# A SwiGLU layer's first column block by seven products instead of eight, and one token sum split where it is made

## The chip, the cores and the metric

One core of a Trainium2 chip runs the whole program. The metric is the device time of one execution in microseconds (us), as the median of several runs.

The names of the engines in the profile: PE is TensorE (matmuls and transposes), DVE is VectorE, ACT is ScalarE, POOL is GpSimd, SP is SyncE, which here only issues DMA transfers, in the order of its queue. Every engine takes its own instructions strictly in order: one that waits holds up all that stand behind it on that engine.

## The reference, cut to what matters

```python
x = x + _rmsnorm(merged @ W['w_out'], W['norm_mix_post'])
f = _rmsnorm(x, W['norm_ffn_pre'])
f = (jax.nn.silu(f @ W['w_ffn_gate']) * (f @ W['w_ffn_up'])) @ W['w_ffn_down']
```

The layer runs on 1024 prompt tokens and on 64 sample tokens (`DEC`); the model width is 1024, the FFN width (`D_FF`) 2816. Everything is float32.

## The kernel before

**Operands.** TensorE works on fp32r operands. A float32 matrix is therefore kept as two fp32r parts, hi and lo: `split` copies the matrix to hi on ACT and subtracts hi from it on DVE to get lo. A product is then three matmuls per 128 rows of the inner width: hi by hi, hi by lo and lo by hi. `wino_mm` issues one such product over 512 of the 1024 inner rows, 12 matmuls of 128x512.

**The output stage (`mix_out`)** goes over nine token tiles in the order 8, 0, 4, 1, 5, 2, 6, 3, 7 (tile 8 holds the 64 sample tokens). For each it multiplies by `w_out`, normalizes (`post`), adds the residual, normalizes again (`pre`, whose result is the tile `xn`), transposes `xn` by eight TensorE transposes into two PSUM banks, and splits them into `H`, the FFN's activation operand: `H[:, k, i, t]` with k the inner rows in eights, i hi or lo, t the token. `block(r, c)` is one quarter of it: 512 inner rows, 512 tokens. While a tile pair (t, t+4) goes through, the hooks of `token_sums` form four sums of those quarters on DVE and put each to `tk`, a tensor in DRAM.

**The FFN's first stage (`ffn_in`)** goes over eleven pieces of 256 columns of `w_ffn_gate` and `w_ffn_up`. For pieces 1 to 10, each matrix is multiplied by seven products in the manner of Strassen and Winograd: two take parts of the weights as they are (a11 and a12), four take sums of weight quarters (s1 to s4, made on POOL by `wino_weights` and then split), one takes a22. Three of the token operands are sums too: T2, T3, T4, which `wino_tokens` loads from `tk` and splits; a fourth, t1, stands in the place of `block(0, 1)` in `H`. The sample tokens' 64 columns go along as `decode_rows`, 16 small matmuls of 128x256 per matrix, which read `HD`, an ACT copy of the sample part of `H`.

Piece 0 is done by `ffn_first` as the plain eight products of each matrix: first all of those on `H`'s tokens 0 to 511 (four output tiles, 96 matmuls, tags wx for gate and wz for up), then those on tokens 512 to 1023. Between the two halves `wino_tokens` brings T2, T3, T4, and at the end of piece 0 it brings t1 from `tk` over `block(0, 1)`, which is free from then on.

**Order.** The instruction order of each engine is fixed when the program is built, by a scheduler that works from its own estimates; nothing is reordered on the chip. Pools that follow each other share memory, so a tile of a new pool may have to wait for the last reader of an old one. Loads and stores all go through SP's one queue.

Of the kernel before, what the change touches and what calls it, by code (L numbers as in the profile page):

```python
# [8 lines left out]
F32 = mybir.dt.float32  # L9
# [59 lines left out]
class Net:  # L69
# [54 lines left out]
    def split(self, wh, wl, raw):  # L124
        self.nc.scalar.activation(wh, raw, AF.Copy)  # L125
        self.nc.vector.tensor_sub(wl, raw, wh)  # L126

# [881 lines left out]
    def pre(self, P, x, gb, hi, lo, hook=None):  # L1009

        nc = self.nc
        r = x.shape[0]
        ss = P.tile([128, 4], F32, "ss", "ss")[:r]
        xn = P.tile([128, D], F32, "xn", "xn")[:r]
        nc.scalar.activation(xn, x, AF.Square, scale=1 / 32.0, accum_out=ss[:, 0:1])
        rs = self.rstd(P.pool, ss[:, 0:1])
        nc.vector.scalar_tensor_tensor(xn, x, rs, gb[:r], op0=OP.mult, op1=OP.mult)
        for k0 in (0, 4):
            ps = self.ps.tile([128, 512], F32, name="tr", tag="tr")
            for k in range(4):  # L1020
                nc.tensor.transpose(ps[:, k * 128:k * 128 + r], xn[:, (k0 + k) * 128:(k0 + k + 1) * 128], self.ident[:r, :r])
            self.split(hi[:, k0:k0 + 4], lo[:, k0:k0 + 4], ps.rearrange("p (k t) -> p k t", k=4)[:, :, :r])
            if hook:
                hook(k0 // 4, ps)

    def token_sums(self, P, t):
# [3 lines left out]
        V = nc.vector  # L1030
        x1, y = [None, None], [None]

        def put(n, x):
            nc.sync.dma_start(self.tk[n, :, :, t * 128:(t + 1) * 128], x.rearrange("p (k t) -> p k t", k=4))

# [4 lines left out]
        def second(r, ps):  # L1040
            if not r:
                y[0] = P.tile([128, 512], F32, "t1", "t1")
                V.tensor_sub(y[0], ps, x1[0])
                put(0, y[0])
                return
            t2 = P.tile([128, 512], F32, "t2", "t2")
            V.tensor_sub(t2, ps, y[0])
            put(1, t2)
            V.tensor_sub(x1[0], t2, x1[0])
            put(2, x1[0])  # L1050
            V.tensor_sub(x1[1], x1[1], t2)
            put(3, x1[1])
        return first, second

# [11 lines left out]
    def mix_out(self, P, U):  # L1066
        nc = self.nc
        self.x2 = self.dram.tile([TOK, D], F32, name="x2")
        self.tk = self.dram.tile([4, 128, 4, 512], F32, name="tk")
        gb, gp = self.bcast(P, "norm_mix_post"), self.bcast(P, "norm_ffn_pre")  # L1070
# [24 lines left out]

    def wino_tokens(self, PT, P, first):

        if first:
            T = [self.H[:, 0:4, :, 512:SEQ]]
        else:  # L1100
            T = [PT.tile([128, 4, 2, 512], F32R, name=f"T{n}") for n in (2, 3, 4)]
            two = lambda t: (t[:, :, 0], t[:, :, 1])
            self.B = dict(b11=self.block(0, 0), b21=self.block(1, 0), b22=self.block(1, 1), t1=self.block(0, 1),
                          t2=two(T[0]), t3=two(T[1]), t4=two(T[2]))
        for i in (0,) if first else (1, 0, 2):
            for k in (0, 2):
                t = T[i][:, k:k + 2, 1].bitcast(F32)
                self.nc.sync.dma_start(t, self.tk[i + (not first), :, k:k + 2])
                for j in range(2):
# [4 lines left out]

    def wino_weights(self, P, w, p, i, sums=True):

# [3 lines left out]
        for r in range(2):  # L1120
            x = W.tile([128, 4, 256], F32, name="raw", tag="wraw", bufs=2) if i % 2 == 0 or not sums else P.tile([128, 4, 256], F32, "raw", "raw")
            nc.sync.dma_start(x, w[:, 4 * r:4 * r + 4, p * 256:(p + 1) * 256])
            if not sums and i == r == 1:
                h, l = (P.tile([128, 4, 256], F32R, n, "s") for n in ("wh", "wl"))
            elif (2 * i + r) % 3 < 2:
# [4 lines left out]
            self.split(h, l, x)  # L1130
            raw.append(x)
            D.append((h, l))
        if not sums:
            return D
        a11, a21 = (raw[0][:, :, s:s + 128] for s in (0, 128))
# [13 lines left out]
        return D, dict(a11=h(D[0], 0), a12=h(D[1], 0), a22=h(D[1], 1), s1=s1, s2=s2, s3=s3, s4=s4)  # L1149

    def ffn_first(self, P, w, HD, PT):

        nc = self.nc
        D = [self.wino_weights(P, w[up], 0, up, sums=False) for up in range(2)]
        g = {}
        for c in range(2):
            for up in range(2):
                for n in range(2):
                    ps = self.ps.tile([128, 512], F32, name="w", tag=("wx", "wz")[up])
                    for r in range(2):  # L1160
                        self.wino_mm(ps, tuple(x[:, :, n * 128:(n + 1) * 128] for x in D[up][r]), self.block(r, c), start=r == 0, stop=r == 1, whole=True)
                    if not up:
                        x = g[f"{n + 1}{c + 1}"] = P.tile([128, 512], F32, "c", f"g{n + 1}{c + 1}")
                        nc.scalar.activation(x, ps, AF.Silu)
                    else:
                        x = g[f"{n + 1}{c + 1}"]
                        nc.vector.tensor_mul(x, x, ps)
                if c:
                    Q = self.ps.tile([128, 512], F32, name="wd", tag="wd")[:, :256]
                    self.decode_rows(Q, self.decode_pairs(HD, D[up]), 0, 16)  # L1170
                    self.decode_gate(P, Q, up, 0)
            if not c:
                self.wino_tokens(PT, P, False)
        self.wino_tokens(PT, P, True)
        self.act_sums(0, g, {x: P.tile([128, 512], F32, "c", "u" + x) for x in ("11", "22", "21")})

# [24 lines left out]

    def wino_mm(self, out, a, b, start=False, stop=True, whole=False):

        for k in range(4):
            for i, j in ((0, 0), (0, 1), (1, 0)):
                self.nc.tensor.matmul(out, a[i][:, k], b[j][:, k], start=start and k == i == j == 0,  # L1206
                                      stop=stop and k == 3 and i == 1, skip_group_check=not start and not whole)

    def ffn_in(self, PT, P):
# [9 lines left out]

        self.ffn_first(P, w, HD, PT)  # L1220
        B = self.B
        for p in range(1, 11):
            for up in range(2):
                D, a = self.wino_weights(P, w[up], p, 2 * p + up)
                X, Y, Z = (self.ps.tile([128, 512], F32, name=t, tag=t) for t in ("wx", "wy", "wz"))
                Q = self.ps.tile([128, 512], F32, name="wd", tag="wd")[:, :256]
                dec = self.decode_pairs(HD, D)
                self.wino_mm(X, a["a11"], B["b11"], start=True)
                self.wino_mm(Y, a["a12"], B["b21"], start=True)
                c = {x: P.tile([128, 512], F32, "c", ("u" if up else "g") + x) for x in ("11", "12", "21", "22") if not (up and x == "12")}  # L1230
                A.activation(c["11"], Y, AF.Copy)
                V.tensor_add(c["11"], c["11"], X)
                self.wino_mm(Z, a["s3"], B["t3"], start=True)
                self.wino_mm(X, a["s2"], B["t2"])
                A.activation(c["21"], X, AF.Copy)
                self.decode_rows(Q, dec, 0, 8)
                self.wino_mm(X, a["s1"], B["t1"])
                A.activation(c["22"], Z, AF.Copy)
                V.tensor_add(c["22"], c["22"], X)  # L1239
                self.decode_rows(Q, dec, 8, 16)  # L1240
                self.wino_mm(X, a["s4"], B["b22"])
                self.wino_mm(Z, a["a22"], B["t4"])
                V.tensor_add(c["21"], c["21"], Z)
                self.decode_gate(P, Q, up, p)
                if not up:
                    g = c
                    A.activation(g["12"], X, AF.Silu)
                    for x in ("11", "22", "21"):
                        A.activation(g[x], g[x], AF.Silu)
                    continue  # L1250
                for x in ("11", "22", "12", "21"):
                    V.tensor_mul(g[x], g[x], X if x == "12" else c[x])
                self.act_sums(p, g, c)
            self.down_sums(P, p)
            if p == 5:
# [356 lines left out]
```

## Time and profile before

| | us |
|---|---|
| median of 3 runs | 1753.33 (1753.03 to 1759.03) |
| the profiled execution's own time | 1759.74 |
| its span, first to last instruction | 1758.0 |
| PE busy in the span | 1693.2 (96%) |
| DVE, ACT, POOL busy | 1036.4, 729.7, 520.9 |

PE is busy nearly all the time, so what counts is how much PE has to do and where it stands still. The places of this case lie between 926 us (the last product of the output stage) and 980 us (the first product of piece 1). Start times are in us from the start of the span.

### The profile page before, as it was taken

The page shows a single profiled execution, that of the slowest core. Times are in us where ns is not written, and L with a number is a line of the kernel's source. Part 1 is how long each engine was busy: PE and PEld are TensorE (multiplying, and loading weights), DVE is VectorE, ACT ScalarE, POOL GpSimd, SP SyncE. Part 2 cuts the span into 40 slices and gives each one's busy share as a digit, 9 for nine tenths or more (in the row PEclk, how much of TensorE's full clock was granted, in tenths as well). Part 3 has the DMA queues.
Part 4 walks back from the last instruction along what each step waited for, and adds up shares of the span by engine and source line. Part 5 has one row for each costly group of instructions (what it writes and reads, how often), then busy time and mean ns, then how long its engine had stood idle before and what let it go on. Part 6 is the DMA issues. An engine that isn't in the chain of part 4 may idle for free.

```text
span 1758.0 us, 24713 instructions
## 1 busy us (share of the span) xinstructions
PE 1693.2 (96%) x9092; PEld 1479.8 (84%) x9092; DVE 1036.4 (59%) x1579; ACT 729.7 (42%) x1355; POOL 520.9 (30%) x450
## 2 busy tenths in 40 slices
PE   8999999999999898899999999999999999999998
PEld 6999998988898877798787888888888877888886
DVE  7437916337777767767464655555555456445674
ACT  6431135125555555633344433333333344444542
POOL 2026200012323223224231544445444212001453
PEclk9999999999999989999999999999999999999999
DMA  8362563884444343147445544446444386655332
GB/s 286 92 153 64 126 137 110 249 213 102 105 102 107 70 109 89 56 151 236 144 157 184 164 140 139 146 133 199 140 140 148 109 302 206 205 189 169 106 110 89
DMA packets 220713, 258.23 MB, mean 147 GB/s; under 512 B 26144, under 2 KB 168592, under 8 KB 220576
## 3 DMA queue, kind: packets, MB, share of 16 engines
q1 hardware_dynamic: 219936, 255.20, 48.0%
q0 software_dynamic: 656, 1.44, 0.6%
q8 instruction: 72, 1.18, 0.3%
q14 instruction: 49, 0.40, 0.1%
HBM read 165.32 MB, written 76.51 MB: 138 GB/s over the span
## 4 chain that ended last, share of the span: by engine, by line
PE 75%; DVE 12%; DMA 5%; ACT 3%; issue 3%; POOL 1%; SPq 1%; DVEq 0%; POOLq 0%; ACTq 0%
PE pj L1206 14%; PE tr L1206 8%; PE pj L137 6%; PE pj L139 6%; PE pj L138 6%; PE z L1372 3%; PE z L1206 3%; DVE p L735 3%; PE pj L1372 3%; PE tr L1372 2%; PE av L811 2%; PE z L138 2%; PE z L139 2%; PE z L137 2%; PE tr L781 1%
## 5 line engine op out<-in xcount | busy, mean ns | idle before, releaser
L137 PE MATMUL pj<-H,wh 128*128 128x362 f32 (+3 forms) x648 | 218.4, 337 | 5.9 <-DVE ql L634 3.6
L139 PE MATMUL pj<-H,wl 128*128 128x362 f32 (+3 forms) x648 | 215.8, 334 | 0.6 <-DVE wl L115 0.6
L138 PE MATMUL pj<-H,wh 128*128 128x362 f32 (+3 forms) x648 | 215.4, 333 | 0.0
L126 DVE TENSOR_TENSOR wl<-raw,wh 128x1024 fp32r<-128x1024 f32 x96 | 136.2, 1422 | 113.0 <-ACT wh L125 109.8
L737 POOL TENSOR_TENSOR w<-w,p 128x383 f32<-128x383 f32 (+4 forms) x68 | 92.7, 1373 | 315.2 <-DVE w L739 187.6
L125 ACT ACTIVATE wh<-raw 128x1024 fp32r<-128x1024 f32 x96 | 101.1, 1058 | 112.7 <-PE z L1372 44.4
L137 PEld LDWEIGHTS pj<-H,wh 128*128 128x128 f32 x648 | 123.3, 190 | 7.6 <-DVE ql L634 3.9
L139 PEld LDWEIGHTS pj<-H,wl 128*128 128x128 f32 x648 | 123.1, 190 | 1.5 <-DVE wl L115 1.0
L138 PEld LDWEIGHTS pj<-H,wh 128*128 128x128 f32 x648 | 123.3, 190 | 0.9 <-issue 0.4
L1206 PE MATMUL pj<-H,s 128*128 128x512 f32 x480 | 118.2, 395 | 0.0
L148 POOL TENSOR_TENSOR rs<-rs,mhalf 128x1 f32<-128x1 f32 (+1 forms) x54 | 32.6, 606 | 279.2 <-DVE rs L147 279.1
L1206 PEld LDWEIGHTS pj<-H,s 128*128 128x128 f32 x480 | 89.9, 188 | 20.9 <-DVE c L1239 0.3
L125 ACT ACTIVATE s<-st 128x512 fp32r<-128x512 f32 x80 | 50.3, 629 | 127.6 <-PE pj L1206 116.8
L1140 POOL TENSOR_TENSOR st<-raw 128x512 f32<-128x512 f32 x40 | 61.3, 1532 | 126.4 <-issue 52.3
L126 DVE TENSOR_TENSOR s<-st,s 128x512 fp32r<-128x512 f32 x80 | 64.4, 805 | 41.5 <-ACT s L125 40.9
L119 ACT ACTIVATE wh<-raw 128x1024 fp32r<-128x1024 f32 (+1 forms) x52 | 46.6, 898 | 98.9 <-PE av L138 51.4
L115 DVE TENSOR_TENSOR wl<-raw,wh 128x1024 fp32r<-128x1024 f32 (+1 forms) x50 | 51.0, 1021 | 57.9 <-ACT wh L119 57.8
L785 ACT ACTIVATE wth<-tr 128x512 fp32r<-128x512 f32 (+2 forms) x112 | 50.3, 453 | 83.3 <-PE tr L781 42.8
L786 DVE TENSOR_TENSOR wtl<-tr,wth 128x512 fp32r<-128x512 f32 (+2 forms) x112 | 55.2, 496 | 49.4 <-ACT wth L785 48.9
L733 ACT ACTIVATE p<-z 128x512 f32<-128x512 f32 (+4 forms) x116 | 59.0, 509 | 42.6 <-PE z L835 16.7
L735 DVE TENSOR_TENSOR_SCAN p<-p,zero 128x384 f32<-128x384 f32 (+4 forms) x68 | 73.9, 1094 | 0.2
L1206 PE MATMUL pj<-H,wh 128*128 128x512 f32 x224 | 71.1, 394 | 0.6 <-ACT H L125 0.4
(553 smaller groups left out, 4626.8 us busy)
## 6 DMA issues: line engine op xcount, KB each, us to landing
sd<-c SPq DMA_DIRECT2D x77, 256.0 KB, 3.1
raw<-sd SPq DMA_DIRECT2D x77, 256.0 KB, 2.8
raw<-in_w_in_dram SPq DMA_DIRECT2D x32, 512.0 KB, 5.4
raw<-in_w_ffn_gate_dram SPq DMA_DIRECT2D x22, 512.0 KB, 3.7
raw<-in_w_ffn_up_dram SPq DMA_DIRECT2D x22, 512.0 KB, 4.8
wd<-in_w_ffn_down_dram SPq DMA_DIRECT2D x44, 256.0 KB, 3.4
td<-wd SPq DMA_DIRECT2D x22, 512.0 KB, 3.1
raw<-td SPq DMA_DIRECT2D x44, 256.0 KB, 3.0
```

Of the source, the lines that this page charges most:

```text
L125: self.nc.scalar.activation(wh, raw, AF.Copy)
L126: self.nc.vector.tensor_sub(wl, raw, wh)
L137: self.nc.tensor.matmul(out, wh, xh, start=i == 0, stop=False)
L138: self.nc.tensor.matmul(out, wh, xl, start=False, stop=False)
L139: self.nc.tensor.matmul(out, wl, xh, start=False, stop=i == n - 1)
L733: nc.scalar.activation(p, z, AF.Sigmoid, scale=-1.0)
L735: nc.vector.tensor_tensor_scan(p[:, ::-1], p[:, ::-1], self.zero.to_broadcast([128, n]), 1.0 if carry is None else carry, op0=OP.mult, op1 ...
L737: (nc.gpsimd if e == 'g' else nc.vector).tensor_tensor(w[:, :n - 1], w[:, :n - 1], p[:, 1:], op=OP.mult)
L786: nc.vector.tensor_sub(wl[:, a:b], ps[:, a:b], wh[:, a:b])
L1140: op(t, x, y)
L1206: self.nc.tensor.matmul(out, a[i][:, k], b[j][:, k], start=start and k == i == j == 0, stop=stop and k == 3 and i == 1, skip_group_check=n ...
L1372: nc.tensor.matmul(B[b + n], x[:, 0, c], y[:, 1], start=new and p == j == 0, stop=p == 10 and j == 2, skip_group_check=not new)
```

## The change

Piece 0 is done by the seven products as well. `ffn_in` is cut into `begin` (the products a11 and a12, which need no sums, and the first output) and `end` (the five others). For piece 0 it runs `begin` for gate, `begin` for up, with the decode rows between the two products, then `wino_tokens` and both `end`s. The sum t1 goes no more through `tk`: the second transposes' first half is not split into `H` (`block(0, 1)` itself is not used any more), and the hook of the output stage splits the sum `y` there instead. `tk` holds three sums.

```diff
 def pre(...):
-            self.split(hi[:, k0:k0 + 4], lo[:, k0:k0 + 4], ps...)
+            if not hook or (hook[1], k0) != (True, 0):
+                self.split(hi[:, k0:k0 + 4], lo[:, k0:k0 + 4], ps...)
...
 def second(r, ps):
                 V.tensor_sub(y[0], ps, x1[0])
-                put(0, y[0])
+                self.split(*(self.H[:, 0:4, i, 512 + t * 128:640 + t * 128] for i in range(2)), four(y[0]))
                 return
...
 def wino_weights(...):
-            x = W.tile(..., tag="wraw", bufs=2) if i % 2 == 0 or not sums else P.tile([128, 4, 256], F32, "raw", "raw")
+            x = W.tile(..., tag="wraw", bufs=2) if i % 2 == 0 else P.tile([128, 4, 256], F32, "raw", "raw")
...
-    def ffn_first(self, P, w, HD, PT):
...
 def ffn_in(...):
+        def begin(p, up):
+            D, a = self.wino_weights(P, w[up], p, 2 * p + up)
...
+            self.wino_mm(X, a["a11"], B[0], start=True)
+            if not p:
+                self.decode_rows(Q, dec, 0, 16)
+            late = self.wino_mm(Y, a["a12"], B[1], start=True)
...
+        for p in range(11):
+            if p:
+                g = end(p, 0, *begin(p, 0)[0], None)
+                end(p, 1, *begin(p, 1)[0], g)
+                self.down_sums(P, p)
+            else:
+                S0, _ = begin(p, 0)
+                S1, late = begin(p, 1)
+                with after(self.last_w[0].ins), after(self.last_w[1].ins):
+                    self.wino_tokens(PT)
+                with after(late.ins):
+                    g = end(p, 0, *S0, None)
+                    end(p, 1, *S1, g)
```

How it stands in the instruction order, at three places. In the rows, `pj`, `z`, `tr` and `av` are PSUM banks, `wh` and `wl` weights' hi and lo, and numbers behind a name tell tiles of one name apart.

PE before, around the transposes of token tile 7, the last of the output stage: the rows of `pj<-H` ahead of them are the 48 matmuls of gate on tokens 0 to 511.

```order
L1206 MATMUL pj<-H,wl 128x512
L1206 MATMUL pj<-H,wh 128x512 x2
L1206 MATMUL pj<-H,wl 128x512
L1021 MATMUL tr<-ident,xn 128x128 x8
L1182 MATMUL z<-wh,HD 128x256
```

PE of the change, from the transposes of token tile 3 to those of tile 7 and the first row behind them: here the only matmuls between the two are the 12 of gate's a11.

```order
L1020 MATMUL tr<-ident,xn 128x128 x8
L1174 MATMUL pj<-H,wh 128x512 x2
L1174 MATMUL pj<-H,wl 128x512
L1174 MATMUL pj<-H,wh 128x512 x2
L1174 MATMUL pj<-H,wl 128x512
L1174 MATMUL pj<-H,wh 128x512 x2
L1174 MATMUL pj<-H,wl 128x512
L1174 MATMUL pj<-H,wh 128x512 x2
L1174 MATMUL pj<-H,wl 128x512
L1020 MATMUL tr<-ident,xn 128x128 x8
L1150 MATMUL z<-wh,HD 128x256
```

The transposes of tile 7 stand 36 matmuls earlier in PE's order than before.

SP's queue of the change at the end of the output stage; `T_9637`, `T_9638` and `T_9639` are T2, T3 and T4, and the first `raw<-in_w_ffn_up_dram` are up's weights of piece 0. Gate's weights of piece 0 are issued early in both kernels, and before, up's stood right behind them.

```order
L1035 DMA tk<-t_9440 512x1x128
L1035 DMA tk<-x_9343 512x1x128
L1035 DMA tk<-x_9352 512x1x128
L1106 DMA T_9637<-tk 128x2x512 x2
L1106 DMA T_9638<-tk 128x2x512 x2
L1120 DMA raw<-in_w_ffn_up_dram 128x4x256 x2
L1106 DMA T_9639<-tk 128x2x512 x2
L1120 DMA raw<-in_w_ffn_gate_dram 128x4x256 x2
```

Up's weights of piece 0 now stand behind the puts of tile 7 and behind four of the six loads of the token sums.

ACT of the change from `HD` on; `s<-st` are the splits of the weight sums, `wh<-raw` those of up's weights.

```order
L1183 ACTIVATE HD<-H 128x1024
L125 ACTIVATE s<-st 128x512 x3
L977 ACTIVATE q<-z 64x256
L125 ACTIVATE s<-st 128x512
L1159 ACT_TABLE_LOAD
L1159 ACTIVATE y<-y 64x256
L125 ACTIVATE wh<-raw 128x1024
L1201 ACTIVATE c<-z 128x512
L125 ACTIVATE wh<-raw 128x1024
L125 ACTIVATE T_9638<-T_9638 128x512 x4
L125 ACTIVATE T_9637<-T_9637 128x512 x4
```

Before, `wh<-raw` followed `HD` at once; now gate's weight sums stand ahead of it, and all splits of the token sums behind it.

## Rows read from the trace of the kernel before

**Rows 1.** Busy time by stretch: span, PE, PEld, DVE, ACT, POOL, clock, DMA

```profile
940.00:960.00 20.00, 17.97 (x89) 14.71 (x88) 12.53 (x19) 12.94 (x21) 0.00 (x0) 1.00 0.78 246
1200.00:1400.00 200.00, 200.00 (x946) 165.53 (x945) 113.18 (x137) 74.57 (x124) 88.83 (x76) 1.00 0.45 144
```

**Rows 2.** Chain that ended last, in order of time: start, us, what

```profile
956.45 10.89 PE pj L1206 x48
967.34 11.15 PE tr L1206 x48
978.50 1.80 PE av L1182 x15
```

**Rows 3.** Timeline of PE: start, us, line, what, [idle before <-releaser]

```profile
928.17 0.49 PE L1206 MATMUL pj<-H,wh 128*128 128x512 f32 x1 [0.39 <-ACT H L125]
928.89 0.50 PE L1206 MATMUL pj<-H,wh 128*128 128x512 f32 x1 [0.23 <-DVE H L126]
...
939.68 1.03 PE L1021 MATMUL tr<-ident,xn 128*128 128x128 f32 x8
942.40 0.38 PE L1182 MATMUL z<-wh,HD 128*128 128x256 f32 x1 [1.68 <-ACT HD L1214]
...
980.13 0.62 PE L1206 MATMUL pj<-H,wh 128*128 128x512 f32 x2
```

**Rows 4.** Timeline of DVE, the chain of token tile 7

```profile
934.79 1.28 DVE L1017 SCALAR_TENSOR_TENSOR xn<-xo,rs,gb_norm_ffn_pre 128x1024 f32<-128x1024 f32 x1 [0.73 <-POOL rs L148]
...
942.75 0.68 DVE L1047 TENSOR_TENSOR t<-tr,t 128x512 f32<-128x512 f32 x1
...
944.68 2.35 DVE L126 TENSOR_TENSOR wl<-raw,wh 128x1024 fp32r<-128x1024 f32 x2
```

**Rows 5.** Timeline of ACT, from the transposes of tile 7 on

```profile
940.32 1.09 ACT L125 ACTIVATE H<-tr 128x512 fp32r<-128x512 f32 x2 [6.46 <-PE tr L1021]
941.29 1.06 ACT L1214 ACTIVATE HD<-H 128x1024 fp32r<-128x1024 f32 x1
942.24 2.01 ACT L125 ACTIVATE wh<-raw 128x1024 fp32r<-128x1024 f32 x2
...
952.73 1.15 ACT L125 ACTIVATE T<-T 128x512 fp32r<-128x512 f32 x2 [6.09 <-DMA T<-tk]
954.09 1.16 ACT L125 ACTIVATE T<-T 128x512 fp32r<-128x512 f32 x2 [0.20 <-DMA T<-tk]
...
958.25 1.16 ACT L125 ACTIVATE T<-T 128x512 fp32r<-128x512 f32 x2 [0.20 <-DMA T<-tk]
```

**Rows 6.** Timeline of SP's queue: puts of tile 7, loads of the sums, weights

```profile
943.46 0.51 SPq L1034 DMA_DIRECT2D tk<-t  x1
947.26 1.91 SPq L1108 DMA_DIRECT2D T<-tk  x4
951.19 0.47 SPq L1122 DMA_DIRECT2D raw<-in_w_ffn_up_dram  x1
```

**Rows 7.** Line 1122, weight loads between 860 and 975 us: from issue to landing

```profile
DMA to landing us min/median/max: 3.5/9.9/11.3
```

**Rows 8.** Busy time by stretch, around two idle times of PE (columns as rows 1)

```profile
372.40:375.80 3.40, 0.01 (x1) 0.01 (x1) 0.60 (x2) 1.68 (x6) 0.00 (x0) 0.87 0.92 191
375.80:382.60 6.80, 6.80 (x27) 6.51 (x28) 3.10 (x6) 0.05 (x1) 3.48 (x7) 0.56 0.74 233
...
589.20:592.00 2.80, 0.10 (x2) 0.07 (x2) 2.79 (x6) 1.97 (x5) 1.15 (x2) 1.00 0.89 205
592.00:596.80 4.80, 4.80 (x23) 4.80 (x24) 3.56 (x7) 1.00 (x3) 0.27 (x1) 0.64 0.01 2
```

**Rows 9.** The page's group of POOL's weight sums: count, busy us, mean ns

```profile
L1140 POOL TENSOR_TENSOR st<-raw 128x512 f32<-128x512 f32 x40 | 61.3, 1532 | 126.4 <-issue 52.3
```

More of the change, by code (lines that the diff above doesn't have):

```diff
@@ L1047, in second @@
             V.tensor_sub(t2, ps, y[0])
-            put(1, t2)
+            put(0, t2)
             V.tensor_sub(x1[0], t2, x1[0])
-            put(2, x1[0])
+            put(1, x1[0])
             V.tensor_sub(x1[1], x1[1], t2)
-            put(3, x1[1])
-        return first, second
+            put(2, x1[1])
+        return (first, False), (second, True)
     def rows(self, dst, prompt, sample, t):
@@ L1093, in mix_out, with wino_tokens @@
             self.pre(P, x, gp, *(self.H[:, :, i, c0:c0 + r] for i in range(2)), hook=hooks.get(t))
[L1096 to L1105, printed above, removed]
+    def wino_tokens(self, PT):
+        T = [PT.tile([128, 4, 2, 512], F32R, name=f"T{n}") for n in (2, 3, 4)]
+        two = lambda t: (t[:, :, 0], t[:, :, 1])
+        self.B = dict(b11=self.block(0, 0), b21=self.block(1, 0), b22=self.block(1, 1), t1=self.block(0, 1),
+                      t2=two(T[0]), t3=two(T[1]), t4=two(T[2]))
+        for i in (1, 0, 2):
             for k in (0, 2):
                 t = T[i][:, k:k + 2, 1].bitcast(F32)
-                self.nc.sync.dma_start(t, self.tk[i + (not first), :, k:k + 2])
+                self.nc.sync.dma_start(t, self.tk[i, :, k:k + 2])
                 for j in range(2):
@@ L1120, in wino_weights @@
         for r in range(2):
-            x = W.tile([128, 4, 256], F32, name="raw", tag="wraw", bufs=2) if i % 2 == 0 or not sums else P.tile([128, 4, 256], F32, "raw", "raw")
+            x = W.tile([128, 4, 256], F32, name="raw", tag="wraw", bufs=2) if i % 2 == 0 else P.tile([128, 4, 256], F32, "raw", "raw")
             nc.sync.dma_start(x, w[:, 4 * r:4 * r + 4, p * 256:(p + 1) * 256])
-            if not sums and i == r == 1:
-                h, l = (P.tile([128, 4, 256], F32R, n, "s") for n in ("wh", "wl"))
-            elif (2 * i + r) % 3 < 2:
+            if (2 * i + r) % 3 < 2:
                 h = W.tile([128, 4, 256], F32R, name="wh", tag="whi", bufs=2)
@@ L1129, in wino_weights @@
                 h, l = P.tile([128, 4, 256], F32R, "wh", "dh"), P.tile([128, 4, 256], F32R, "wl", "dl")
-            self.split(h, l, x)
+            self.last_w = self.split(h, l, x)
             raw.append(x)
             D.append((h, l))
-        if not sums:
-            return D
         a11, a21 = (raw[0][:, :, s:s + 128] for s in (0, 128))
@@ L1149, in wino_weights @@
         return D, dict(a11=h(D[0], 0), a12=h(D[1], 0), a22=h(D[1], 1), s1=s1, s2=s2, s3=s3, s4=s4)
-    def ffn_first(self, P, w, HD, PT):
[L1153 to L1175, printed above, removed]
     def decode_pairs(self, HD, D):
@@ L1200, in decode_gate, with wino_mm @@
         nc.sync.dma_start(self.ad[p * 256:(p + 1) * 256].rearrange("(i p) t -> p i t", p=128), o)
-    def wino_mm(self, out, a, b, start=False, stop=True, whole=False):
+    def wino_mm(self, out, a, b, start=False, stop=True):
         for k in range(4):
             for i, j in ((0, 0), (0, 1), (1, 0)):
-                self.nc.tensor.matmul(out, a[i][:, k], b[j][:, k], start=start and k == i == j == 0,
-                                      stop=stop and k == 3 and i == 1, skip_group_check=not start and not whole)
+                x = self.nc.tensor.matmul(out, a[i][:, k], b[j][:, k], start=start and k == i == j == 0,
+                                      stop=stop and k == 3 and i == 1, skip_group_check=not start)
+        return x
     def ffn_in(self, PT, P):
@@ L1218, in ffn_in @@
         w = [self.I[n][0].rearrange("(k p) n -> p k n", p=128) for n in ("w_ffn_gate", "w_ffn_up")]
[L1220 to L1235, printed above, removed]
+        def begin(p, up):
+            D, a = self.wino_weights(P, w[up], p, 2 * p + up)
+            X, Y = (self.ps.tile([128, 512], F32, name=t, tag=t) for t in ("wx", "wy"))
+            Q = self.ps.tile([128, 512], F32, name="wd", tag="wd")[:, :256]
+            dec = self.decode_pairs(HD, D)
+            B = self.block(0, 0), self.block(1, 0)
+            self.wino_mm(X, a["a11"], B[0], start=True)
+            if not p:
+                self.decode_rows(Q, dec, 0, 16)
+            late = self.wino_mm(Y, a["a12"], B[1], start=True)
+            c = {x: P.tile([128, 512], F32, "c", ("u" if up else "g") + x) for x in ("11", "12", "21", "22") if not (up and x == "12")}
+            A.activation(c["11"], Y, AF.Copy)
+            V.tensor_add(c["11"], c["11"], X)
+            if not p:
+                self.decode_gate(P, Q, up, p)
+            return (a, X, Q, dec, c), late
@@ L1236, in ffn_in, with end @@
+        def end(p, up, a, X, Q, dec, c, g):
+            B = self.B
+            Z = self.ps.tile([128, 512], F32, name="wz", tag="wz")
+            self.wino_mm(Z, a["s3"], B["t3"], start=True)
+            self.wino_mm(X, a["s2"], B["t2"])
+            A.activation(c["21"], X, AF.Copy)
+            if p:
                 self.decode_rows(Q, dec, 0, 8)
-                self.wino_mm(X, a["s1"], B["t1"])
-                A.activation(c["22"], Z, AF.Copy)
-                V.tensor_add(c["22"], c["22"], X)
+            self.wino_mm(X, a["s1"], B["t1"])
+            A.activation(c["22"], Z, AF.Copy)
+            V.tensor_add(c["22"], c["22"], X)
+            if p:
@@ L1251, in ffn_in @@
[L1251 to L1254, printed above, removed]
+            if not up:
+                A.activation(c["12"], X, AF.Silu)
+                for x in ("11", "22", "21"):
+                    A.activation(c[x], c[x], AF.Silu)
+                return c
+            for x in ("11", "22", "12", "21"):
+                V.tensor_mul(g[x], g[x], X if x == "12" else c[x])
```

30 lines of the change are left out of this document (14 added, 16 removed).

## The prediction

> **What bounds the kernel now.** I read the busy time by stretch first: from 1200 to 1400 us, deep in the FFN's pieces, PE is busy for all of 200 us [rows 1]. There a product more or less moves the end by its own length, and whatever is lost before carries through to the end. Around the change it is not quite so: from 940 to 960 us PE works 17.97 of 20 us [rows 1]. So the question is when PE begins piece 1, and I went from there to the timelines of PE, of the engines it waits for, and of SP's queue.
>
> The timeline of PE [rows 3] shows piece 0 beginning at 928.17 us and piece 1 at 980.13: 51.96 us. The two sizes needed are in the chain of work [rows 2]: 48 matmuls of 128x512 take 10.89 and 11.15 us, so 12 (one product) take 2.75 us; 15 decode matmuls take 1.80, so 16 take 1.92. The 192 matmuls, 32 decode matmuls and 8 transposes of piece 0 are then 44.1 + 3.8 + 1.0 = 48.9 us; the other 3 are waits, the longest of them 1.68 us for `HD`.
>
> Why are there so few waits, when tile 7's normalization is still going on? Its `xn` is finished at 934.79 + 1.28 = 936.07 us [rows 4], but its transposes come at 939.68 [rows 3], behind 48 matmuls which need nothing of tile 7. Up's weights are in SBUF long before: their copy to hi runs on ACT as soon as `HD` is out of the way [rows 5]. The 96 matmuls on the first 512 tokens and then the 48 of gate on the others cover the way of the token sums through DRAM.
>
> **The change part by part.**
>
> *Matmuls.* Seven products of 12 for each matrix instead of eight: 24 matmuls fewer, 2 x 2.75 = 5.5 us of PE. This is the whole of the gain.
>
> *Wait for tile 7.* Ahead of its transposes stand now 12 matmuls, not 48. They begin at 928.17 as before and contain the 0.49 us before the second matmul (928.89 less 928.17, less its 0.23) [rows 3], and end at 928.17 + 2.75 + 0.49 = 931.4. `xn` comes at 936.07 at the earliest, since DVE's and ACT's order up to it is the same. PE stands 4.7 us, and the transposes end at 937.1.
>
> *Wait for `HD`.* Before, `HD` was ready 942.35 - 939.68 = 2.7 us behind the transposes' start [rows 3, 5]. Now the first H split waits for the subtraction of `y`, an operation of 0.68 us like its neighbour [rows 4]: 936.1 + 2.7 + 0.7 = 939.5. PE stands 2.4 us. Then gate's decode rows and its a12 product, 1.92 + 2.75, until 944.1.
>
> *Wait for up's weights.* Next on PE is up's a11, and its weights' load now stands in SP's queue behind the puts of tile 7 and four token loads. Before, the put of the second sum was issued at 943.46, 3.8 us behind the start of the transposes, and the first token load that reads it at 947.26, again 3.8 us later [rows 3, 6]. DVE has as many operations ahead of that sum as before. So: 936.1 + 3.8 + 3.8 = 943.7 for the first token load, and as four of them took 1.91 us to issue [rows 6], 945.6 for up's. Then it queues for bandwidth. The first token load landed 5.5 us after its issue (952.73 less 947.26), the second 1.4 us later, the fifth at 958.25: 5.5 us for four loads of 512 KB, each of which ACT waited for [rows 5, 6]. As up's first half is the fifth load here, it lands 5.5 us behind the first. For the first I take the mean of 5.5 us and the 3.5 of the fastest weight load [rows 7], since fewer puts stand before it: 943.7 + 4.5 + 5.5 = 953.7. The copy to hi takes half of 2.01 us, 1.06 with its end [rows 5]: up's a11 begins at 954.8. PE stands 954.8 - 944.1 = 10.7 us. Bounds: 953.8 and 955.8 with 3.5 or 5.5 us for the first load; 945.6 + 3.5 + 1.06 = 950.2 if up's load does not queue at all.
>
> *The rest of piece 0* is up's a11, decode rows, up's a12 and the ten products of both `end`s: 144 matmuls, 33.0 us, and 1.92. The lo part of up's weights is ready 1.2 us behind the hi part (half of 2.35 [rows 4]), while only two products' matmuls and one decode matmul can run without it: 0.6 us more. Piece 1 begins, in PE work done, at 954.8 + 33.0 + 1.9 + 0.6 = 990.3 us instead of 980.13: **10.2 us later**. In other words, 18.4 us of waits are added, 5.5 of work and about 3 of old waits are removed.
>
> *The clock.* After PE had stood 3.4 us from 372.4, the granted clock of the next 6.8 us was 0.56 of full speed, mostly the 1.2 GHz level; after 2.8 us from 589.2, 0.64 for 4.8 us [rows 8]. The first costs 6.8 x 0.44 = 3.0 us of PE's work, the second 1.7. The waits of 4.7 and 10.7 us are longer than both. What is lost after the first lies inside the wait for up's weights (even at half speed gate's decode rows and a12 end at 939.5 + 9.3 = 948.8); what is lost after the second counts: 2.4 us, between 1.7 and 3.0.
>
> *What costs nothing.* The eight sums of piece 0 are POOL work of 1.53 us each [rows 9], while POOL did nothing from 940 to 960 [rows 1]; gate's four and their splits stand before up's copies, which wait for their load anyway, and up's four are needed only after gate's products. Without this cover one sum with its splits would cost some 3 us once. t1's way through `tk`, now gone (four puts, two loads, four splits), lay under up's products; its split in the output stage replaces one of the same size. The token sums no longer decide: T3's splits follow up's copies, and PE needs T3 only 8 us after up's a11 begins.
>
> Sum: 10.2 + 2.4 = **12.6 us slower**. The profiled execution (1759.74, span 1758.0) would become 1772; it lies 6.4 us over the median of the runs, which has none of this stage in it that I can name, so I add the difference to the median: 1753.33 + 12.6 = 1765.9.
>
> **A rule weighed.** The steady 1.4 us between landings [rows 5] is what makes up's load late. The Trainium skill, *DMA: Bandwidth & Descriptors*, section *Queues, rings and completion order*, says that each DMA engine takes descriptors in ring order, which agrees; it also says that completion is not first in, first out per issuing engine, and that a later transfer can finish before an earlier one. No landing out of order is in these rows. By the second sentence the early landing of the first rival would be possible; by the first it would not.
>
> **The rivals.**
>
> *Up's load does not queue.* It lands 3.5 us after issue like the fastest weight load [rows 7]; up's a11 starts at 950.2, and piece 1 at 950.2 + 35.5 = 985.7: 5.6 us, with the clock's 1.7 it is 7.3: 1760.6. Against it: in the trace loads issued in a row landed at the pace of the bandwidth [rows 5].
>
> *The loss is covered, no slower.* If up's weights are split by 944.1, the third wait is gone, with its clock loss; piece 1 begins at 944.1 + 34.9 = 979.0, 1.1 us earlier: 1752. For this the load must be issued by about 939.5 (944.1 less 1.06 and 3.5), so ahead of the token loads. For it: SP has nothing to do from tile 7's store until its puts. Against it: SP's order. It also shows why a real gain is unlikely: the waits for tile 7 and `HD` alone take 7.1 us, more than the 5.5 saved.
>
> *A further wait.* The order interleaves piece 1's first products with piece 0's `end`, and both need loads that stand behind T4; if those land as late as a load 11.3 us after issue [rows 7], or the clock stays low over several stretches, some 5 us come on top: 1771. Against it: piece 1's first weights used are the tenth load, which would land at 953.7 + 5 x 1.4 = 960.7; PE comes to them three products after up's a12, at 954.8 + 8.0 + 8.3 = 971.1.
>
> **How the numbers follow.** Forecast (1763 to 1768): 0.60. No queueing: 0.15. Covered: 0.12. Further wait: 0.13. Half a per cent, 8.8 us, is about what a measurement of this kernel can tell; the runs shown already lie 6 us apart. The range of 1757 to 1771 leaves out the covered case and the upper half of the last one. Slower by over 0.5% (from 1762.1): nearly all of the forecast and the last, 0.72. Within: covered and not queued, 0.24. Faster by over 0.5%: 0.04, since all the saved work is 5.5 us.
>
> **What would show it.** In the profile after: 168 matmuls of 128x512 in piece 0; PE idle some 4.7 us ahead of tile 7's transposes, released by DVE's `xn`; about 2 us for `HD`; about 10 us before up's a11, released by ACT or DVE on `wh` and `wl`, behind a DMA wait of ACT on up's `raw`; a low granted clock after it. The prediction is wrong if up's `raw` lands before 948 us, if PE has other work in that wait, or if piece 1 meets waits of its own.

## The result, and the profile after

| | before | after |
|---|---|---|
| median | 1756.7 us (6 runs, 1753.03 to 1759.03) | 1770.8 us (6 runs, 1768.77 to 1773.03) |
| ratio after to before | | 1.0083, 95% interval 1.0069 to 1.0096 |
| the profiled execution's span | 1758.0 | 1767.0 |

The change makes the kernel 14.1 us slower, between 12.1 and 16.9 by the interval; the sum of the prediction was 12.6. The three runs that the prediction started from had a median of 1753.33; with three more it is 1756.7. So 1765.9 was forecast, in 1763 to 1768, and 1770.8 was measured.

The two profiled executions did not reach the changed stage at the same time (in the profiles of this case the row below starts anywhere between 920.4 and 929.6 us), so I lay them together at the last Square of the output products, on ACT. Before:

```profile
926.94 0.60 ACT L987 ACTIVATE xo<-z 128x512 f32<-128x512 f32 x1 [4.71 <-PE z L139]
```

The same row after the change:

```profile
921.96 0.60 ACT L986 ACTIVATE xo<-z 128x512 f32<-128x512 f32 x1 [4.75 <-PE z L138]
```

From this row to the end it was 1758.0 - 926.94 = 831.1 us before and 1767.0 - 921.96 = 845.0 now: 14.0 us more, all of the difference. To compare a start time after with one before, add 5.0.

What PE waited for after the change, between 926 and 1000 us (us in total, times, longest):

```profile
PE pj L1174 <- ACT wh L125: 8.4, 1, 8.4
PE tr L1020 <- DVE xn L1016: 5.5, 1, 5.5
PE z L1150 <- ACT HD L1183: 2.0, 1, 2.0
```

These are the three waits of the prediction, in the places that it named, and this stretch has no others; they were forecast at 10.7, 4.7 and 2.4 us. The timeline of PE, with the rows that answer to [rows 3]:

```profile
932.20 1.94 PE L1020 MATMUL tr<-ident,xn 128*128 128x128 f32 x8 [5.51 <-DVE xn L1016]
936.16 0.58 PE L1150 MATMUL z<-wh,HD 128*128 128x256 f32 x1 [2.02 <-ACT HD L1183]
...
951.13 1.22 PE L1174 MATMUL pj<-H,wh 128*128 128x512 f32 x2 [8.37 <-ACT wh L125]
```

Up's a11 begins 18.9 us behind the start of the transposes; 18.7 were forecast. The chain of work that ended last shows the way between them (it answers to [rows 2]; start, us, what):

```profile
929.77 2.29 DVE xn L1016
...
932.20 1.10 PE tr L1020 x4
...
936.62 2.58 DMA tk<-t
...
941.36 8.64 DMA raw<-in_w_ffn_up_dram
950.02 1.07 ACT wh L125
...
951.13 1.22 PE pj L1174 x2
```

SP's queue, which answers to [rows 6]:

```profile
936.62 0.52 SPq L1035 DMA_DIRECT2D tk<-t  x1
937.35 1.20 SPq L1035 DMA_DIRECT2D tk<-x  x2
939.26 2.01 SPq L1106 DMA_DIRECT2D T<-tk  x4
941.36 1.48 SPq L1120 DMA_DIRECT2D raw<-in_w_ffn_up_dram  x2
```

Up's weights stand behind three puts and four token loads, and take 8.64 us from issue to landing. The row of DVE that answers to the first of [rows 4] is the one that the prediction did not see coming:

```profile
929.77 2.27 DVE L1016 SCALAR_TENSOR_TENSOR xn<-xo,rs,gb_norm_ffn_pre 128x1024 f32<-128x1024 f32 x1 [0.73 <-POOL rs L147]
```

`xn` starts at its old time (929.77 + 5.0 = 934.8), but it takes 2.27 us instead of 1.28. Before, POOL did nothing from `xn`'s start on for 29.43 us (timeline of POOL):

```profile
964.18 1.29 POOL L1140 TENSOR_TENSOR st<-raw 128x512 f32<-128x512 f32 x1 [29.43 <-DMA raw<-in_w_ffn_gate_dram]
```

Now it makes its first weight sums at that very time:

```profile
929.71 3.47 POOL L1134 TENSOR_TENSOR st<-raw 128x512 f32<-128x512 f32 x2
```

Over the whole program one such sum takes POOL no longer than before; the page's group, which answers to [rows 9], now holds 44 of them:

```profile
L1134 POOL TENSOR_TENSOR st<-raw 128x512 f32<-128x512 f32 x44 | 64.0, 1454 | 104.2 <-issue 48.1
```

The granted clock, by stretch (columns as in rows 1), answers to [rows 8]:

```profile
929.70:939.90 10.20, 5.68 (x25) 5.31 (x26) 8.12 (x10) 3.62 (x6) 5.97 (x5) 0.50 0.22 62
946.80:951.00 4.20, 0.00 (x0) 0.00 (x0) 0.00 (x0) 0.98 (x1) 0.87 (x1) 0.50 1.08 367
951.00:957.00 6.00, 5.87 (x14) 4.37 (x15) 5.89 (x6) 5.97 (x12) 4.52 (x3) 0.50 0.90 304
957.00:977.00 20.00, 20.00 (x96) 16.44 (x95) 13.44 (x21) 9.48 (x17) 2.91 (x2) 1.00 0.23 69
```

Behind each of the two long waits the granted clock is at half, 1.2 GHz. The 5.87 us of work after 951 are worth 2.9 us at full speed. From 957 to 1000 PE neither waits nor runs slowly, so piece 1 meets no wait of its own.

### The profile page after: what moved, and what is told of

Same layout as the page of the kernel before. It is cut to its first block, busy times and chain, and to the rows that moved or that the text cites. A ratio compares the mean times of both kernels' runs of the same rounds, so it can differ in the third digit from the quotient of the medians.

```text
span 1767.0 us, 24693 instructions
## 1 busy us (share of the span) xinstructions
PE 1689.6 (96%) x9068; PEld 1474.9 (83%) x9068; DVE 1047.8 (59%) x1589; ACT 735.1 (42%) x1365; POOL 533.4 (30%) x458
## 4 chain that ended last, share of the span: by engine, by line
PE 73%; DVE 12%; DMA 7%; issue 3%; ACT 3%; POOL 1%; SPq 1%; DVEq 0%; POOLq 0%; ACTq 0%
PE pj L1174 14%; PE tr L1174 7%; PE pj L136 6%; PE pj L138 6%; PE pj L137 6%; PE z L1365 3%; PE z L1174 3%; DVE p L734 3%; PE pj L1365 3%; PE tr L1365 2%; PE av L810 2%; PE z L137 2%; PE z L138 2%; PE z L136 2%; PE tr L780 2%
## 5 line engine op out<-in xcount | busy, mean ns | idle before, releaser
L1174 PE MATMUL pj<-H,s 128*128 128x512 f32 x528 | 130.1, 395 | 0.0
L1174 PEld LDWEIGHTS pj<-H,s 128*128 128x128 f32 x528 | 98.7, 188 | 22.7 <-DVE c L1217 0.3
L125 ACT ACTIVATE s<-st 128x512 fp32r<-128x512 f32 x88 | 55.1, 628 | 137.6 <-PE pj L1174 122.0
L125 DVE TENSOR_TENSOR s<-st,s 128x512 fp32r<-128x512 f32 x88 | 69.9, 796 | 50.2 <-ACT s L125 49.4
L734 DVE TENSOR_TENSOR_SCAN p<-p,cy,zero 128x512 f32<-128x512 f32 (+1 forms) x48 | 55.2, 1156 | 24.5 <-ACT p L732 24.5
```

Source lines behind the costliest of these rows:

```text
L125: return self.nc.scalar.activation(wh, raw, AF.Copy), self.nc.vector.tensor_sub(wl, raw, wh)
L734: nc.vector.tensor_tensor_scan(p[:, ::-1], p[:, ::-1], self.zero.to_broadcast([128, n]), 1.0 if carry is None else carry, op0=OP.mult, op1 ...
L1174: x = self.nc.tensor.matmul(out, a[i][:, k], b[j][:, k], start=start and k == i == j == 0, stop=stop and k == 3 and i == 1, skip_group_che ...
```

## The experiments

The theory: the loss is one chain, from `xn` of tile 7 over its transposes, its sums and puts and the token loads to the load of up's weights; waits that lie beside this chain add nothing. The rivals: the three waits add; the clock makes the difference; or the token sums would hold PE up anyway. Ratios are to the kernel before, with their 95% interval; the changed kernel's is 1.0083.

| run | median us | ratio |
|---|---|---|
| up_first | 1764.2 | 1.0038 (1.0024 to 1.0053) |
| sums_after_xn | 1767.7 | 1.0069 (1.0054 to 1.0085) |
| idle_products | 1769.3 | 1.0075 (1.0062 to 1.0089) |
| decode_early | 1767.9 | 1.0063 (1.0049 to 1.0078) |
| three_mends | 1763.0 | 1.0042 (1.0029 to 1.0055) |
| up_on_act_queue | 1763.1 | 1.0044 (1.0030 to 1.0057) |
| up_in_wout_place | 1757.7 | 1.0009 (0.9999 to 1.0019) |
| t2_t3_kept | 1757.2 | 1.0013 (0.9998 to 1.0027) |
| sums_last | 1756.6 | 1.0009 (0.9995 to 1.0023) |

**up_first: up's load ahead of the token loads.**

```diff
-            nc.sync.dma_start(x, w[:, 4 * r:4 * r + 4, p * 256:(p + 1) * 256])
+            self.last_raw = nc.sync.dma_start(x, w[:, 4 * r:4 * r + 4, p * 256:(p + 1) * 256])
...
-                with after(self.last_w[0].ins), after(self.last_w[1].ins):
+                with after(self.last_raw.ins), after(self.last_w[0].ins), after(self.last_w[1].ins):
                     self.wino_tokens(PT)
```

> The changed kernel with one line more: the loads of the token sums T2, T3, T4 are queued on SP behind up's weights of piece 0, which were behind four of them. Theory (the loss is mostly the wait for up's weights, and that wait is SP's order): up's load is issued some 3 us earlier, at about 938.5 on the changed kernel's time axis, and lands after about 4 us instead of 8.6, as only the puts stand before it; its first product begins at about 943.6 instead of 951.1, and less of it runs at the low clock. The time falls by 7.5 to 10 us, to 1761 to 1763. Rival (the wait only moves to the token sums, which now land later): the first product with T3 waits in its place, and the time falls by less than 3 us.

The time fell by 6.6 us: less than the theory's 7.5 to 10, and more than the rival's 3. The longest waits of PE, 926 to 1000 us (the profiled execution took 1771.45 us, 7 more than the median, so only its waits and order are read):

```profile
PE tr L1020 <- DVE xn L1016: 5.5, 1, 5.5
PE z L1150 <- ACT HD L1183: 2.0, 1, 2.0
PE pj L1174 <- ACT wh L125: 0.8, 1, 0.8
PE pj L1174 <- DVE wl L125: 0.6, 1, 0.6
```

The wait for up's weights shrank from 8.4 to 1.4 us, while the other two stayed; waits of 0.5 us for `y` and 0.2 for another `wl` are new. The order of SP's queue alone is worth some 6.6 us.

**sums_after_xn: POOL's sums behind `xn` of tile 7.** An operation on one column of `xn` holds POOL back.

```diff
+        if hook and hook[1]:
+            self.behind_xn = nc.gpsimd.tensor_add(ss[:, 3:4], xn[:, D - 1:D], xn[:, D - 1:D])
...
-                S0, _ = begin(p, 0)
-                S1, late = begin(p, 1)
+                with after(self.behind_xn.ins):
+                    S0, _ = begin(p, 0)
+                    S1, late = begin(p, 1)
```

> The changed kernel, with POOL reading one column of each normalized tile of token tiles 4 to 7 before it goes on, so that gate's first weight sums begin only when DVE has finished xn of tile 7 (in the changed kernel the two run at the same time, and that xn took 2.27 us, where it took 1.28 before). Theory (POOL's sums slow DVE's operation down): xn takes 1.28 us again, tile 7's transposes come about 1.0 us earlier, and so does all behind them; the time falls by about 1 us, too little for the timing, so the rows decide. Rival (xn is slow for another reason): it stays at 2.3 us.

DVE's row is as before the change:

```profile
932.56 1.28 DVE L1016 SCALAR_TENSOR_TENSOR xn<-xo,rs,gb_norm_ffn_pre 128x1024 f32<-128x1024 f32 x1 [0.73 <-POOL rs L147]
```

The wait for `xn` fell from 5.5 to 4.5 us, and the median by 3.1. That POOL's sums stretched `xn` by 1.0 us is shown. The other 2 us are not explained by a row: from the last Square to the end this profile has 844.2 us and the changed kernel's 845.0, so with four runs of this kernel they may be chance.

**idle_products: products that nobody reads, in the waits.** 24 matmuls in the wait for `xn` and 36 in that for up's weights keep PE at work; the outputs of the kernel stay the same.

```diff
+                F = self.ps.tile([128, 512], F32, name="fill", tag="wd")
+                for _ in range(2):
+                    self.wino_mm(F, a["a12"], B[1], start=True)
+                with self.tc.issue_after(late.ins):
+                    F = self.ps.tile([128, 512], F32, name="fill", tag="wz")
+                    for _ in range(3):
+                        self.idle = self.wino_mm(F, a["a12"], B[1], start=True)
```

> The changed kernel with 60 matmuls more whose results nothing reads, the same a12 product over and over into spare PSUM banks: 24 before tile 7's transposes and 36 behind gate's a12, where PE waits 5.5 and 8.4 us. Theory (part of the loss is the clock that falls in these waits): the granted clock stays at 2.4 GHz, tile 7's transposes take 1.0 us instead of 1.9, up's a11 runs at 0.23 us a matmul instead of 0.43; with PE doing 14 us more, the time falls by about 3 us, to 1767 to 1768. Rival (the clock costs nothing, as what it slows is waiting anyway): no change, or a rise where the extra matmuls do not fit into the waits.

The median is 1.5 us lower, which the two intervals do not tell from no change. The clock was low for 3.4 us instead of 20.4, by stretch:

```profile
933.40:936.80 3.40, 2.93 (x13) 2.93 (x14) 3.40 (x7) 1.98 (x4) 0.57 (x1) 0.51 0.49 136
936.80:946.80 10.00, 10.00 (x47) 8.34 (x47) 2.51 (x3) 2.71 (x4) 1.03 (x1) 1.00 0.88 267
```

So a full clock gives back little here, 1.5 us by the medians and 0.1 by the profiles (844.9 us for 845.0 from the last Square to the end), and not the 14: the clock is not the cause of the loss. Up's a11 begins 29.2 us behind that Square in both, and of the 2.9 us that the low clock took behind it, waits of 1.1 us for `y` and 0.7 us for `wl`, which the slower PE had not met, took back 1.8.

**decode_early: `HD` copied right behind tile 8.** `HD` takes the place of `HS`, whose last reader is tile 8's product.

```diff
+            if t == 8:
+                self.HD = self.PY.tile([128, 8, 2 * DEC], F32R, name="HD", tag="HS")
+                nc.scalar.activation(self.HD.rearrange("p k (i t) -> p k i t", i=2), self.H[:, :, :, SEQ:], AF.Copy)
```

> The changed kernel with HD copied in the output stage, right behind token tile 8, into the memory of the operand that tile 8 used. PE's order then has gate's decode rows, a11 and a12 all ahead of tile 7's transposes, so that the waits of 5.5 us for xn and 2.0 us for HD are filled. Up's load stays behind four token loads. Theory (what sets the end is the chain xn, transposes, sums, puts, token loads, up's load; the first two waits lie beside it): up's a11 begins at the same time but for the 0.9 us by which the transposes run at full clock, the wait before it grows to some 16 us, and the time falls by 1 us at most, to 1769.8 to 1771. Rival (the three waits add up, as the sum on record has them): it falls by 7 us, to 1763 to 1764.

The waits of PE in the same stretch:

```profile
PE pj L1177 <- ACT wh L125: 16.5, 1, 16.5
PE tr L1020 <- DVE xn L1016: 1.2, 1, 1.2
```

6.3 us of waiting are gone and 8.1 have come back in the wait for up's weights: the waits do not add, they lie beside the chain. The gain of 2.9 us is more than the theory's upper end of 1, and far from the rival's 7. Tile 7's transposes now run at full clock (timeline of PE):

```profile
933.38 1.06 PE L1020 MATMUL tr<-ident,xn 128*128 128x128 f32 x8 [1.15 <-DVE xn L1016]
```

Up's a11 starts 17.5 us behind them instead of 18.9. The 1.4 us are there at the first put of tile 7 already, which is issued 3.0 us behind the transposes' start and not 4.4: the transposes take 1.06 us instead of 1.94, and DVE's order has one split of 0.6 us less ahead of the sum that is put. That `HD` is no longer copied there plays no part in it, since in the changed kernel its copy stood behind the splits that DVE waits for.

**three_mends: the edits of up_first, sums_after_xn and decode_early together.** Up's first load is written ahead of `begin`:

```diff
+        self.raw_up = [P.tile([128, 4, 256], F32, "raw", "raw") for _ in range(2)]
+        for r in range(2):
+            self.last_raw = nc.sync.dma_start(self.raw_up[r], w[1][:, 4 * r:4 * r + 4, 0:256])
```

> The changed kernel with three edits together: up's first weights are put on SP's queue ahead of the token-sum loads, HD is copied right after tile 8, and POOL's weight sums of piece 0 wait until xn of tile 7 is there. Theory (the three costs lie on one chain, and taking up's load off the queue is worth most; the other two add what they take away once that load is no longer last): from up_first's 1764.2, less 1.0 for xn, 2.0 for the wait for HD and up to 0.8 for the rest of the wait for up's weights, plus up to 1 because the products now come sooner to the token sums: 1760.5 to 1762. Rival A (after up_first the token sums T2 to T4 set the end, whatever else is taken away): 1763.5 to 1765. Rival B (the three gains add, 6.6 + 3.1 + 2.9): 1758.

No gain by the ratio over up_first. The time is next to rival A's, but its reason is not: PE stands on up's weights, not on the token sums (waits of PE):

```profile
PE pj L1182 <- ACT wh L125: 11.2, 1, 11.2
```

And the load is still issued late, right behind the puts (SP's queue):

```profile
934.76 0.52 SPq L1037 DMA_DIRECT2D tk<-t  x1
936.81 1.20 SPq L1037 DMA_DIRECT2D tk<-x  x2
938.09 1.28 SPq L1198 DMA_DIRECT2D raw<-in_w_ffn_up_dram  x2
```

**up_on_act_queue: the same load from ACT's queue**, where no put stands ahead of it (`nc.scalar.dma_start` in the three lines above).

> The same three edits, but up's first weights are issued from ACT's queue, behind tile 7's first split, so that they stand behind no put and the token-sum loads stand behind no weight load. Theory: no wait of PE is left but that for xn of tile 7 (about 4.5 us), and the token sums come 1 to 2 us sooner than in three_mends: 1758.5 to 1761, still above the kernel before, by the wait for xn less 5.5 us of products, plus what the clock costs after it. Rival A (the token sums or ACT and DVE, which make their splits, set the end): within 1 us of three_mends. Rival B (the two transfers slow each other and up's weights land late again): slower than three_mends by 2 us or more.

No change: the time is rival A's, within 1 us of three_mends, but again its reason is not. PE stands on up's weights:

```profile
PE pj L1182 <- ACT wh L125: 13.5, 1, 13.5
```

The timeline of ACT, with its DMA issues (ACTq):

```profile
931.62 0.42 ACTq L1198 DMA_DIRECT2D raw<-in_w_ffn_up_dram  x1
931.82 0.62 ACT L125 ACTIVATE H<-t 128x512 fp32r<-128x512 f32 x1
937.92 0.45 ACTq L1198 DMA_DIRECT2D raw<-in_w_ffn_up_dram  x1
938.41 0.63 ACT L125 ACTIVATE s<-st 128x512 fp32r<-128x512 f32 x1 [5.98 <-DMA tk<-x]
```

The first half of up's weights goes out at 931.62, the second only at 937.92: ACT stood still until the puts of tile 7 had read their tiles. No queue held this load back; its memory did. The `raw` tiles of `ffn1` lie in memory that the output stage's pool held before, and the second comes free only when a put of tile 7 has read it.

**up_in_wout_place: another place for up's first weights.** `next_pool` closes `w_out`'s pool and opens a small one in its place, and `raw`, `dh` and `dl` move into it. Tile 7's products have read `w_out`'s first slabs by 918.86 us, when the load is issued.

```diff
+            if t == 7:
+                self.PT = self.next_pool()
+                self.raw_up = [self.PT.tile([128, 4, 256], F32, name="raw", tag="raw", bufs=2) for _ in range(2)]
+                for h in range(2):
+                    self.last_raw = nc.sync.dma_start(self.raw_up[h], w[:, 4 * h:4 * h + 4, 0:256])
             self.post(P, f, gb, xr, x, x)
```

> three_mends, with the memory of up's first weights moved: their raw tiles and the split dh, dl lie in the place of w_out's first two slabs, which is free when tile 7's products are half done, and no longer in the output stage's own memory, which is free only after tile 7's token sums (in three_mends the load is issued at 938.09, right behind those sums and their puts). Theory (the rest of the loss, 11.2 us of waiting ahead of up's a11, hangs on that memory): the load lands before tile 7's transposes, up's a11 follows them at once, and the next wait is for the token sums T3 and T2, about 5 us long: 1763 - 6 = 1757, in 1755.5 to 1758.5, no longer to be told from the kernel before. Rival (the token sums, not up's weights, have set the end since up_first, and take the whole wait over): 1761 to 1763.

5.3 us less than three_mends, and not to be told from the kernel before. The waits of PE:

```profile
PE tr L1188 <- ACT T L125: 8.3, 1, 8.3
PE pj L1188 <- DVE T L125: 0.6, 1, 0.6
```

Up's products now run ahead of tile 7's transposes, and the wait for `xn` is gone with that for the weights. Now the token sums are what is late, with 8.3 us where I had expected 5.

**t2_t3_kept: T2 and T3 without DRAM for the last tiles.** The loads of their first three quarters move up to tile 7's products, and the last quarter is split from the sums themselves.

```diff
-            put(0, t2)
+            own = lambda n, s: self.split(*(self.T[n][:, :, i, 384:] for i in range(2)), four(s)) if t == 3 else put(n, s)
             V.tensor_sub(x1[0], t2, x1[0])
-            put(1, x1[0])
+            own(1, x1[0])
+            own(0, t2)
```

> up_in_wout_place, and T2 and T3 also lie in w_out's place: their first three quarters are loaded while tile 7's products still run, and the quarter of tiles 3 and 7 is split straight from the sums, without DRAM; only T4 still goes the old way. Theory (the put, the load and the wait for them are what is left of the cost): the wait for T3 falls from about 5 us to 1 or 2, and the 5.5 us of products saved come through: 1752 to 1755, faster than the kernel before by 1 to 4 us. Rival (DVE, which must make eight more splits of 0.5 us between xn of tile 7 and the end of its sums, becomes what is waited for): 1756 to 1759.

The wait for T is gone, and nothing was won; the rival held. The waits of PE:

```profile
PE av L1176 <- DVE wl L125: 3.3, 1, 3.3
PE tr L1200 <- DVE s L125: 1.6, 1, 1.6
PE tr L1200 <- ACT s L125: 1.3, 1, 1.3
```

DVE is busy for all of the 12.5 us from 934 to 946.5, with rows that are far longer than they need be:

```profile
932.18 4.13 DVE L125 TENSOR_TENSOR T<-T 128x384 fp32r<-128x384 f32 x4
936.23 2.28 DVE L125 TENSOR_TENSOR wl<-raw,wh 128x1024 fp32r<-128x1024 f32 x1
```

**sums_last: POOL's sums behind the token sums.** As sums_after_xn, but the operation that holds POOL back reads the last token sum.

```diff
-            V.tensor_sub(x1[1], x1[1], t2)
+            self.last_sum = V.tensor_sub(x1[1], x1[1], t2)
+            self.behind_sum = self.nc.gpsimd.tensor_add(self.ss3, x1[1][:, 511:512], x1[1][:, 511:512])
```

> t2_t3_kept, with POOL's weight sums of piece 0 put behind the last token sum of tiles 3 and 7 and not behind xn of tile 7. In t2_t3_kept four splits of T3 took 4.13 us and a split of up's weights 2.28 while POOL ran its first sums; four splits of T2 took 1.95 and up's other split 1.22 or less where POOL was idle. Theory (POOL slows DVE, and DVE is what PE now waits for): those rows go back to 1.95 and 1.2, DVE is 3.2 us earlier at its last token sum, PE's wait for wl of 3.3 us nearly goes, and the time falls by 1 to 3 us: 1754.5 to 1756.5. Rival (the weight sums come too late, s3 is what PE then waits for): the wait for s grows from 2.9 us to 5 or more, and the time is 1757 or above.

The rows of DVE went where the theory put them:

```profile
934.17 1.96 DVE L125 TENSOR_TENSOR T<-T 128x384 fp32r<-128x384 f32 x4
936.05 1.22 DVE L125 TENSOR_TENSOR wl<-raw,wh 128x1024 fp32r<-128x1024 f32 x1
```

But PE now waits for the weight sums, as the rival had it, and the time, 1756.6 us, is what it was:

```profile
PE tr L1201 <- ACT s L125: 6.3, 2, 5.2
```

None of the nine beats the kernel before. The last three come to its time within the measurement.

## Which steps of the prediction failed, and which held

**The direction and the mechanism held.** Three waits of PE replace the work saved, in the places named, the longest for up's weights behind the token loads in SP's queue. The rivals of an early landing and of a covered loss are out. The number was off: 1770.8 us lies 2.8 above the forecast's 1763 to 1768. It is next to the 1771 of the rival of a further wait, but by chance: no wait of piece 1 is in the rows. Two terms were wrong.

**The base failed: 1753.33 us measured 1756.7.** That is 3.4 of the 4.9 us between forecast and measurement. "I add the difference to the median" took a median of three runs, and three runs more moved it by 3.4 us. The sum against the profiled execution, 1772, came nearer, also by chance: that execution took 3.0 us more than the median of six runs.

**The weight sums on POOL failed: put at nothing, they cost 1.0 us.** "What costs nothing" called the eight sums of piece 0 hidden because POOL had been idle and their results are needed late. The rows that it went by start at 940 us; the first two sums run from 934.7 on that axis, beside DVE's `xn`, and stretch it from 1.28 to 2.27 us, at the head of the chain. "`xn` comes at 936.07 at the earliest, since DVE's and ACT's order up to it is the same" looked at the order and not at what runs beside it. With that the transposes start 1.1 us later than forecast (932.20 + 5.0 = 937.2 for 936.1), and up's a11 another 0.2 later. sums_after_xn shows the 1.0. This is most of the 1.4 us by which the sum was short in the profiles.

From up's a11 on the sum was right to 0.1 us: 951.13 + 35.5 + 2.4, and the 777.9 from piece 1 to the end (1758.0 - 980.13), make 1766.9 for a span of 1767.0. This is partly luck: the clock took 2.9 us there instead of 2.4, and the 0.6 us of waiting for `wl` did not come, since PE at half clock was too slow to meet it.

**The single waits were right only as a chain.** 18.7 us from the transposes to up's a11 were forecast and 18.9 came: up's load was issued 9.2 us behind the transposes' start for 9.5, and took 8.6 us for 8.1. The split of PE's standing was less exact: `xn` 5.5 for 4.7, `HD` 2.0 for 2.4, up's weights 8.4 for 10.7, the last also because gate's decode rows ran at half clock and so took up some of the time. decode_early shows that the terms of `xn` and `HD` are no costs of their own, and idle_products that the clock's is not one in full.

**What the prediction had as the reason for the late load was half of it.** "SP's order" is worth 6.6 of the 14 us (up_first). Behind it stands the memory of `raw`, which the prediction did not look at: up_on_act_queue has no queue to blame and is as slow as three_mends, and up_in_wout_place, with other memory, wins 5.3 over it. The covered rival asks that "the load must be issued by about 939.5": in up_on_act_queue the second of its tiles came free 16.8 us behind the last Square, which is 943.7 on that axis. Before the change this did not matter: up's first weights lay in tiles of another pool (the diff's line in `wino_weights` moves them) and their loads went out at 848 us.

**Why the 5.5 us never come through.** With up's weights early, PE stands 8.3 us for T3, which must go through DRAM behind tile 7; without DRAM, 6.2 us for the splits of up's weights and of the weight sums; with DVE undisturbed, 6.3 us for the weight sums. The kernel before had all 192 matmuls of piece 0 to do while this happened, none of which needs a sum; the changed one has 48, a11 and a12 of both matrices. Each mend lays bare the next chain, and they are of about the same length. Whether a version without any of these waits would be faster than before was not tried.

## What to carry to other kernels

Work that needs nothing late is worth more than its price at the seam of two stages: count what the removed matmuls were covering before counting their time. For a load that should come early ask for two things, its place in the queue and whose memory its tile inherits, since the second binds as hard and shows only as a wait for somebody else's put. An idle engine is not a free one when its operations share something with the engine that heads the chain; look which of their rows would lie side by side.

## What the runs showed of the hardware

**DVE and POOL hold each other up, by whole operations.** Three cases. In the changed kernel POOL's first sum begins at 929.71 and `xn` at 929.77. One sum takes 1.25 us where nothing disturbs it (two took 2.50 in sums_after_xn), so it would end at 930.96; `xn`'s own 1.28 us from there make 932.24, and it ended at 932.04. POOL's second sum then waits in its turn: 1.25 us from 932.04 make 933.29, and the two sums ended at 933.18. In up_in_wout_place DVE's split `wl` of up's weights met POOL's residual sum:

```profile
924.49 3.11 DVE L125 TENSOR_TENSOR wl<-raw,wh 128x1024 fp32r<-128x1024 f32 x1
...
932.00 1.22 DVE L125 TENSOR_TENSOR wl<-raw,wh 128x1024 fp32r<-128x1024 f32 x1
```

```profile
924.11 2.41 POOL L991 TENSOR_TENSOR xo<-xo,xr 128x1024 f32<-128x1024 f32 x1 [1.57 <-ACT wh L125]
```

POOL is done at 926.52; 1.22 us from there, what the second half took alone, make 927.74, and the row ended at 927.60. In sums_last it went the other way: POOL's operation on a single column, 0.19 us in sums_after_xn, met six of DVE's splits in a row, from 940.78 to 943.95:

```profile
941.01 2.99 POOL L1056 TENSOR_TENSOR ss<-x 128x1 f32<-128x1 f32 x1 [8.08 <-DVE x L1055]
```

It ended at 944.00, when they did. In each case the one that came second ended as if it had begun only when the other was done, to within 0.2 us. The Trainium skill, *SBUF — State Buffer*, section *Who interferes with whom*, has this as a rule: VectorE and GpSimd share one pair of ports, which is an exclusive lock, an operation of VectorE with two inputs in SBUF contends with one of GpSimd that reads SBUF, and the order of issue decides which is blocked. The three cases agree with it; `xn` and these splits all have two inputs in SBUF. A prediction that drew on it could have had the 1.0 us in its sum.

**The clock stays low for a while after work is back.** Behind the wait for up's weights the granted clock was 0.50 (1.2 GHz) until 957, nearly 6 us after PE's first matmul.
